# Linear attention: decay factors multiplied in place over 128 partitions, and half of each key tile copied by ScalarE

## The chip, the core and the metric

The program runs on one core of a Trainium2 chip. The metric is the device time of one execution in microseconds (us). Engines: PE is TensorE (matmuls; PEld its weight loads), DVE is VectorE, ACT is ScalarE, POOL is GpSimd, SP issues the DMAs.

## What is computed

Two blocks of a small model on 256 tokens of width 1024. The first block has two layers; each has three branches (softmax attention, pooling, gated linear attention), merged by gates. The change is in the linear attention, which the reference writes as a scan over chunks with a decay for each key dimension:

```python
def gla_scan(q, k, v, log_a, s0, with_out):
    ...
    def step(s, inp):
        qq, kk, vv, aa = inp
        b = jnp.cumsum(aa, axis=2)
        ...
        inter = jnp.einsum('bhcd,bhde->bhce', qq * jnp.exp(b), s)
        decay = jnp.exp(jnp.where(mask, b[:, :, :, None, :] - b[:, :, None, :, :], -jnp.inf))
        attn = jnp.einsum('bhid,bhjd,bhijd->bhij', qq, kk, decay)
        intra = jnp.einsum('bhij,bhje->bhie', attn, vv)
        return s_new, inter + intra

    _, o_f = gla_scan(q, k, v, af, sc_f, True)
    _, o_b = gla_scan(flip(q), flip(k), flip(v), flip(ab), sc_b, True)
```

There are 4 heads of 64 key dimensions and 128 value dimensions, a forward and a backward direction, and a context sequence of 256 tokens ahead of the 256 main ones.

## The kernel before

Activations lie transposed: 128 features on the partitions, tokens along the row (columns 0 to 255 the context, 256 to 511 the main sequence). Layer 0 works on all 512 columns, layer 1 on the main 256 alone (`lo` is 0 or 256). All large matmuls are three products of rounded halves: `split` has ACT cast a weight tile from `raw` to `wh` (L425) and DVE, or POOL for every fourth tile, subtract it to get `wl` (L427).

One head of linear attention (`gla_head`) puts both directions in one tile: partitions 0 to 63 hold the forward decay sums, 64 to 127 the backward ones (`U`, and `Rr` shifted by one token). The queries and keys of two heads share a tile (`q2`, `k2`), so a head's 64 rows are the upper or the lower half (`rows`). The causal product is cut in eight levels (`lv`): at each, every block of 2s tokens (s = 1 to 128) has an upper and a lower half, and queries of the one meet keys of the other. A level makes `E`, the exponentials of the distances to the block's middle (two subtractions on DVE, L1136 and L1137, and one exponential on ACT, L1138), and multiplies it with q and k into four quarters (L1140 to L1143): queries into `Z` (one of three buffers `zb`) and keys into `K_` (one of eight, `kz`), whose other quarters were set to zero once for each layer (L1187). Each multiplication covers 64 partitions and half the columns; two run on POOL and two on DVE:

```python
            ef.tensor_mul(v4(Z, 1, f), v4(E, 1, f), v4(qs, 1, rows))
            ef.tensor_mul(v4(K_, 0, f), v4(E, 0, f), v4(ks, 0, rows))
            ew.tensor_mul(v4(Z, 0, w_), v4(E, 0, w_), v4(qs, 0, rows))
            ew.tensor_mul(v4(K_, 1, w_), v4(E, 1, w_), v4(ks, 1, rows))
```

One level later `cross` multiplies `K_` with `Z` on PE (`plv`, L1111 and L1105) and DVE or ACT puts the product into place under a mask. At a head's start a product without decay (`pd`, L1081) and the state of the context (`ek`, L1066 to L1074, transposed on PE as `pst`, L1089) are made.

A head yields after each level, and `weave` puts the matmuls of the merge and of the pooling branch (`z_merge`, `pbr`, `z_pool_x`) between the yields. A scheduling layer then fixes one order for each engine; the engines take their instructions strictly in that order.

Of the kernel before, what the change touches and what calls it, by code (L numbers as in the profile page):

```python
# [674 lines left out]
def trunk(b, l, xs, st, A):  # L675

    nc, S = b.nc, b.S
# [4 lines left out]
    q0 = 0 if full else 256  # L682
# [16 lines left out]
    if st is None:  # L699
# [3 lines left out]
        for s_ in range(2):  # L703
            acc, t = S.cols(256), S.cols(256)
# [48 lines left out]
    def win2(name, t, cols):  # L753
        return win_pair((name, t), (name, t + 1), cols, cols)
# [6 lines left out]
    q2, k2, gv, la = [], [], [], []  # L761
# [131 lines left out]
    def silu2(ps):  # L893

        g = S.cols(NQ)
        nc.scalar.activation(g.ap, ps[:, QC], AF.Tanh, scale=0.5)
        nc.vector.scalar_tensor_tensor(g.ap, g.ap, 1.0, ps[:, QC], ALU.add, ALU.mult)
        return g
# [146 lines left out]

    def gla_head(hd):
        rows = slice(64 * (hd % 2), 64 * (hd % 2) + 64)
        qs, ks = q2[hd // 2], k2[hd // 2]
        U, Rr = la[hd], S.get()
        tot = b.sm.tile([P, 2], F32, tag="tot", name="tot")  # L1050
        A, Ao = S.get(), S.get()
        for s_ in range(2):
            c = slice(256 * s_, 256 * s_ + 256)
# [12 lines left out]
        ek = S.get()  # L1066
        nc.scalar.activation(ek[:, 0:256], U[:, 0:256], AF.Exp, bias=bias[:, 0:1], scale=b.c("sgn")[:, 0:1])
        nc.scalar.activation(ek[:, 256:512], U[:, 256:512], AF.Exp, bias=bias[:, 1:2], scale=b.c("sgn")[:, 2:3])
        for d in range(2):
            o = slice(64 * d, 64 * d + 64)  # L1070
            eng = nc.gpsimd if o == rows else nc.vector
            eng.tensor_mul(ek[o, 0:256], ek[o, 0:256], ks[rows, 0:256])
            eng.tensor_mul(ek[o, 256:512], ek[o, 256:512], qs[rows, 256:512])

        pd = b.pb.tile([P, 512], F32, tag="p", name="pd")
        tiles = [t for t in range(4) if t // 2 in seqs]
# [1 line left out]
        blocks = [(t, hb) for t in tiles for hb in range(2)]  # L1078
        for t, hb in blocks:
            j = slice(t * P + 64 * hb, t * P + 64 * hb + 64)  # L1080
            nc.tensor.matmul(pd[64 * hb:64 * hb + 64, t * 64:t * 64 + 64], ks[rows, j], qs[rows, j], start=True, stop=True)  # L1081
        Ad = Ao[:, lo // 2:256]
        nc.scalar.mul(Ad, pd[:, lo // 2:256], 2.0)
        yield
# [1 line left out]
        def state():  # L1086
            ps = b.pb.tile([P, 512], F32, tag="p", name="pst")
            for t in range(2):
                nc.tensor.transpose(ps[:, t * P:(t + 1) * P], ek[:, t * P:(t + 1) * P], b.ident)  # L1089
            nc.scalar.copy(ek[:, 0:256], ps[:, 0:256])  # L1090
            yield
            for t in range(2):
                nc.tensor.matmul(ps[:, 256:384], ek[:, t * P:(t + 1) * P], gv[t][:, hd * P:(hd + 1) * P],
                                 start=t == 0, stop=t == 1)
            nc.scalar.copy(ek[:, 0:P], ps[:, 256:384])
            yield

        def cross(lv):
            ps = b.pb.tile([P, 512], F32, tag="p", name="plv")
            Z, K_ = b.zb[lv % 3], b.kz[lv]  # L1100
            t64 = lambda t_: t_.rearrange("p (t i) -> p t i", i=64)
            if lv == 7:
                for t in tiles:
                    j = (t ^ 1) * P
                    nc.tensor.matmul(ps[:, t * P:(t + 1) * P], K_[:, j:j + P], Z[:, t * P:(t + 1) * P], start=True, stop=True)  # L1105
                nc.scalar.copy(Ao[:, lo:], ps[:, lo:])
                return
            for t, hb in blocks:
                j = t * P + 64 * hb
                i = j if lv < 6 else t * P + 64 * (1 - hb)  # L1110
                nc.tensor.matmul(ps[64 * hb:64 * hb + 64, t * 64:t * 64 + 64], K_[:, j:j + 64], Z[:, i:i + 64],  # L1111
                                 start=True, stop=True)
            src = ps[:, lo // 2:256]
            if lv < 6:
                mk = b.mask[:, lv * 64:(lv + 1) * 64].unsqueeze(1).broadcast_to((P, n // P, 64))
                nc.vector.copy_predicated(t64(Ad), mk, t64(src))
                src = Ad
            if lv > 4:
                for hb in range(2):
                    rr, o = slice(64 * hb, 64 * hb + 64), 64 * (hb if lv == 5 else 1 - hb)  # L1120
                    nc.scalar.copy(A[rr, lo:].rearrange("p (t i) -> p t i", i=P)[:, :, o:o + 64], t64(src)[rr])

        n = 512 - lo
        st_ = state()
        f, w_ = slice(0, 64), slice(64, 128)
        ef, ew = (nc.gpsimd, nc.vector) if hd % 2 == 0 else (nc.vector, nc.gpsimd)
        for lv in range(8):
            s = 1 << lv
            nb = n // (2 * s)
            E = S.get()  # L1130

            def v4(t_, half, o=slice(0, P)):
                return t_[o, lo:].rearrange("p (m h s) -> p m h s", h=2, s=s)[:, :, half]

            mid = Rr[:, lo:].rearrange("p (m c) -> p m c", c=2 * s)[:, :, s:s + 1].broadcast_to((P, nb, s))
            nc.vector.tensor_sub(v4(E, 0), mid, v4(U, 0))  # L1136
            nc.vector.tensor_sub(v4(E, 1), v4(U, 1), mid)  # L1137
            nc.scalar.activation(E[:, lo:], E[:, lo:], AF.Exp, scale=1.0 / TAU)  # L1138
            Z, K_ = b.zb[lv % 3], b.kz[lv]
            ef.tensor_mul(v4(Z, 1, f), v4(E, 1, f), v4(qs, 1, rows))  # L1140
            ef.tensor_mul(v4(K_, 0, f), v4(E, 0, f), v4(ks, 0, rows))
            ew.tensor_mul(v4(Z, 0, w_), v4(E, 0, w_), v4(qs, 0, rows))
            ew.tensor_mul(v4(K_, 1, w_), v4(E, 1, w_), v4(ks, 1, rows))  # L1143
            S.put(E)
            next(st_, None)
            if lv:
                cross(lv - 1)
            yield
        S.put(U, Rr)
        o_ = S.cols(NQ)  # L1150

        def tail():
# [29 lines left out]

    def gla_chain():
        gla_decay()
        b.kz, b.zb = [S.get() for _ in range(8)], [S.get() for _ in range(3)]
        for t in (*b.kz, *b.zb):
            nc.gpsimd.memset(t, 0.0)  # L1187
        yield
        outs, norm = [], iter(())
        for hd in range(4):  # L1190
            steps = gla_head(hd)
            while True:
                try:
                    next(steps)
                except StopIteration as e:
                    o_, norm = e.value
                    outs.append(o_)
                    break
                next(norm, None)
                yield  # L1200
        for _ in norm:
            yield
        S.put(*q2, *k2, *gv, *b.kz, *b.zb)
        for p2 in range(2):
            for i, ps in enumerate(win2("gla_gate", 2 * p2, QC)):
                g = silu2(ps)
                o_ = outs[2 * p2 + i]
                nc.vector.scalar_tensor_tensor(g.ap, o_.ap, 0.5, g.ap, ALU.mult, ALU.mult)  # L1208
                S.drop(o_)
                ygla.append(g)  # L1210
# [25 lines left out]

    weave(mla_chain(), 14, cat(mla_gates(), turns(mods(), gla_cols())), 15 if full else 11)
    weave(gla_chain(), 46, cat(merge(0, ymla), pooling(), merge(1, ypool)), 24)
    if full:
        b.lo_every = 1 << 30  # L1240
# [880 lines left out]
```

## Time and profile before

| | |
|---|---|
| three runs | 1535.64 us median (1535.45 to 1537.04) |
| the profiled execution | 1536.71 us, span 1534.9 us |
| busy share of the span | PE 93%, PEld 79%, DVE 70%, ACT 46%, POOL 28% |
| mean granted TensorE clock | 0.96 of full speed |
| linear attention with its filler | about 258 to 440 us (layer 0) and 770 to 925 us (layer 1) of the span |

The span runs from the first to the last instruction of the profiled execution. PE is busy nearly throughout, so what can move the time is where PE stands still or runs at a lower clock, and what the other engines do there.

### The profile page before, as it was taken

How to read it: one execution, taken by the hardware profiler on the slowest of the kernel's cores; microseconds unless marked ns; L12 is line 12 of the kernel's file. 1: busy time of each engine (PE TensorE's matmuls, PEld its weight loads, DVE VectorE, ACT ScalarE, POOL GpSimd, SP SyncE). 2: the span in 40 equal slices, each digit the busy share in tenths (PEclk: the TensorE clock that was granted, in tenths of full speed). 3: DMA queues.
4: the chain of work that ended last, by engine and by line, in shares of the span. 5: the costliest groups of instructions: out<-in, count | busy, mean ns of one | idle time of the engine just before them, and what ended most of it. 6: DMA issues, size and time to landing. Idle time of an engine off the chain costs nothing. (4 is left out here: it accounts for less than half of the span.)

```text
span 1534.9 us, 27423 instructions
## 1 busy us (share of the span) xinstructions
PE 1427.4 (93%) x10700; PEld 1212.0 (79%) x10700; DVE 1070.7 (70%) x2113; ACT 713.5 (46%) x1307; POOL 433.8 (28%) x428
## 2 busy tenths in 40 slices
PE   5999999999899999899998899979899999799997
PEld 1676776777788788886877789978668999699997
DVE  4455557877779865755589876758988549698843
ACT  3434445343433764454454445633532435366642
POOL 1010003445341004520035341344644003521212
PEclk8999999999999999999989999978999999799999
DMA  9534440321133363335024335844221325266660
GB/s 358 185 109 141 134 149 17 104 76 56 45 94 117 130 197 99 97 110 165 19 79 124 91 111 172 266 141 125 78 84 37 98 62 169 74 206 181 179 187 32
DMA packets 61041, 187.91 MB, mean 122 GB/s; under 512 B 7024, under 2 KB 8560, under 8 KB 60912
## 3 DMA queue, kind: packets, MB, share of 16 engines
q1 hardware_dynamic: 60912, 186.17, 38.5%
q8 instruction: 84, 1.38, 0.4%
q14 instruction: 45, 0.37, 0.1%
HBM read 180.11 MB, written 6.03 MB: 121 GB/s over the span
## 5 line engine op out<-in xcount | busy, mean ns | idle before, releaser
L425 ACT CAST wh<-raw 128x1024 fp32r<-128x1024 f32 (+1 forms) x296 | 279.4, 949 | 255.9 <-PE y L442 50.6
L427 DVE TENSOR_TENSOR wl<-raw,wh 128x1024 fp32r<-128x1024 f32 (+1 forms) x225 | 263.1, 1170 | 163.9 <-ACT wh L425 160.9
L427 POOL TENSOR_TENSOR wl<-raw,wh 128x1024 fp32r<-128x1024 f32 (+1 forms) x71 | 144.6, 2037 | 641.9 <-ACT wh L425 624.8
L442 PE MATMUL z_merge<-s,wh 128*128 128x512 f32 (+1 forms) x768 | 199.6, 350 | 0.0
L442 PEld LDWEIGHTS z_merge<-s,wh 128*128 128x128 f32 x768 | 135.5, 197 | 17.4 <-issue 1.5
L442 PE MATMUL z_merge<-s,wl 128*128 128x512 f32 (+1 forms) x384 | 133.0, 346 | 0.0
L442 PE MATMUL pbr<-s,wh 128*128 128x256 f32 (+1 forms) x512 | 120.6, 327 | 2.9 <-ACT s L432 2.0
L442 PE MATMUL pup<-s,wh 128*128 128x256 f32 x656 | 118.5, 283 | 0.1
L442 PEld LDWEIGHTS pup<-s,wh 128*128 128x128 f32 x656 | 102.5, 192 | 0.2 <-ACT wh L425 0.2
L442 PE MATMUL y<-s,wh 128*128 128x256 f32 x496 | 99.6, 297 | 0.0
L442 PEld LDWEIGHTS pbr<-s,wh 128*128 128x128 f32 x512 | 86.8, 192 | 12.3 <-ACT s L432 2.6
L442 PE MATMUL pwo<-s,wh 128*128 128x256 f32 (+1 forms) x448 | 91.4, 302 | 2.3 <-ACT s L1251 1.7
L442 PE MATMUL pup<-s,wl 128*128 128x256 f32 x328 | 92.8, 283 | 0.0
L442 PEld LDWEIGHTS y<-s,wh 128*128 128x128 f32 x496 | 79.8, 196 | 7.4 <-issue 4.9
L442 PE MATMUL pbr<-s,wl 128*128 128x256 f32 (+1 forms) x256 | 83.1, 325 | 0.0
L442 PEld LDWEIGHTS z_merge<-s,wl 128*128 128x128 f32 x384 | 75.9, 198 | 8.5 <-issue 0.8
L442 PEld LDWEIGHTS pwo<-s,wh 128*128 128x128 f32 x448 | 73.1, 194 | 5.5 <-ACT s L1251 1.9
L1138 ACT ACTIVATE s<-s 128x512 f32<-128x512 f32 (+1 forms) x64 | 33.3, 524 | 89.1 <-DVE s L1137 77.9
L442 PE MATMUL y<-s,wl 128*128 128x256 f32 x248 | 71.7, 289 | 0.0
L432 ACT CAST s<-s 128x256 fp32r<-128x256 f32 (+1 forms) x88 | 42.6, 487 | 57.1 <-DVE s L1208 14.3
L442 PE MATMUL pwo<-s,wl 128*128 128x256 f32 (+1 forms) x224 | 67.6, 302 | 1.5 <-DVE wl L427 1.5
L442 PE MATMUL pdn<-s,wh 128*128 128x256 f32 x352 | 63.4, 283 | 0.0
(490 smaller groups left out, 3545.7 us busy)
## 6 DMA issues: line engine op xcount, KB each, us to landing
raw<-wts SPq DMA_DIRECT2D x294, 512.0 KB, 4.3
s<-wts SPq DMA_DIRECT2D x57, 256.0 KB, 5.1
s5t<-s SPq DMA_DIRECT2D x16, 256.0 KB, 2.0
s<-s5t SPq DMA_DIRECT2D x16, 256.0 KB, 3.3
s<-xc SPq DMA_DIRECT2D x8, 256.0 KB, 5.3
x<-xc SPq DMA_DIRECT2D x8, 256.0 KB, 5.0
s<-tabs SPq DMA_DIRECT2D x4, 256.0 KB, 3.8
out<-s SPq DMA_DIRECT2D x8, 128.0 KB, 1.8
```

The costliest lines, as they stand in the source:

```text
L425: self.nc.scalar.copy(hi[:, :n], src)
L427: self.last_lo = eng.tensor_sub(lo[:, :n], src, hi[:, :n])
L432: self.nc.scalar.copy(hi, src)
L442: self.nc.tensor.matmul(ps, u, v[:, cols], start=start and n == 0, stop=stop and n == last)
L1138: nc.scalar.activation(E[:, lo:], E[:, lo:], AF.Exp, scale=1.0 / TAU)
```

## The change

The 64 rows of q and k that belong to a head are first copied by ACT into two full tiles: `KQ` has k on partitions 0 to 63 and q on 64 to 127, `QK` the other way round (four copies of 64 partitions for each head). A level then multiplies `E` in place over all 128 partitions, the one half of its columns with `KQ`, the other with `QK`, in two DVE instructions. `E` itself serves as `Z`; in the quarters that were zero it now holds products that the zeros of `K_` or the mask cancel. ACT copies the two key quarters from `E` into `K_`. POOL has no work left in the levels. The three `zb` buffers and their six memsets go; `E` is freed after the matmuls of its level. The four multiplications of `ek` (L1072, L1073) now read `KQ` and `QK`: DVE does the context half of the columns, POOL the main half. `pd` reads `KQ` and `QK` instead of `k2` and `q2`.

```diff
--- before.py
+++ after.py
@@ -1045,7 +1045,13 @@
 
     def gla_head(hd):
         rows = slice(64 * (hd % 2), 64 * (hd % 2) + 64)
-        qs, ks = q2[hd // 2], k2[hd // 2]
+        f, w_ = slice(0, 64), slice(64, 128)
+
+        KQ, QK = S.get(), S.get()
+        for t_, (a, c) in ((KQ, (k2, q2)), (QK, (q2, k2))):
+            for o, src in ((f, a), (w_, c)):
+                c0 = q0 if src is q2 else 0
+                nc.scalar.copy(t_[o, c0:], src[hd // 2][rows, c0:])
         U, Rr = la[hd], S.get()
         tot = b.sm.tile([P, 2], F32, tag="tot", name="tot")
         A, Ao = S.get(), S.get()
@@ -1068,9 +1074,9 @@
         nc.scalar.activation(ek[:, 256:512], U[:, 256:512], AF.Exp, bias=bias[:, 1:2], scale=b.c("sgn")[:, 2:3])
         for d in range(2):
             o = slice(64 * d, 64 * d + 64)
-            eng = nc.gpsimd if o == rows else nc.vector
-            eng.tensor_mul(ek[o, 0:256], ek[o, 0:256], ks[rows, 0:256])
-            eng.tensor_mul(ek[o, 256:512], ek[o, 256:512], qs[rows, 256:512])
+            kt_, qt_ = (KQ, QK) if d == 0 else (QK, KQ)
+            nc.vector.tensor_mul(ek[o, 0:256], ek[o, 0:256], kt_[o, 0:256])
+            nc.gpsimd.tensor_mul(ek[o, 256:512], ek[o, 256:512], qt_[o, 256:512])
 
         pd = b.pb.tile([P, 512], F32, tag="p", name="pd")
         tiles = [t for t in range(4) if t // 2 in seqs]
@@ -1078,7 +1084,7 @@
         blocks = [(t, hb) for t in tiles for hb in range(2)]
         for t, hb in blocks:
             j = slice(t * P + 64 * hb, t * P + 64 * hb + 64)
-            nc.tensor.matmul(pd[64 * hb:64 * hb + 64, t * 64:t * 64 + 64], ks[rows, j], qs[rows, j], start=True, stop=True)
+            nc.tensor.matmul(pd[64 * hb:64 * hb + 64, t * 64:t * 64 + 64], KQ[f, j], QK[f, j], start=True, stop=True)
         Ad = Ao[:, lo // 2:256]
         nc.scalar.mul(Ad, pd[:, lo // 2:256], 2.0)
         yield
@@ -1097,19 +1103,21 @@
 
         def cross(lv):
             ps = b.pb.tile([P, 512], F32, tag="p", name="plv")
-            Z, K_ = b.zb[lv % 3], b.kz[lv]
+            Z, K_ = Es.pop(0), b.kz[lv]
             t64 = lambda t_: t_.rearrange("p (t i) -> p t i", i=64)
             if lv == 7:
                 for t in tiles:
                     j = (t ^ 1) * P
                     nc.tensor.matmul(ps[:, t * P:(t + 1) * P], K_[:, j:j + P], Z[:, t * P:(t + 1) * P], start=True, stop=True)
                 nc.scalar.copy(Ao[:, lo:], ps[:, lo:])
+                S.put(Z)
                 return
             for t, hb in blocks:
                 j = t * P + 64 * hb
                 i = j if lv < 6 else t * P + 64 * (1 - hb)
                 nc.tensor.matmul(ps[64 * hb:64 * hb + 64, t * 64:t * 64 + 64], K_[:, j:j + 64], Z[:, i:i + 64],
                                  start=True, stop=True)
+            S.put(Z)
             src = ps[:, lo // 2:256]
             if lv < 6:
                 mk = b.mask[:, lv * 64:(lv + 1) * 64].unsqueeze(1).broadcast_to((P, n // P, 64))
@@ -1122,8 +1130,7 @@
 
         n = 512 - lo
         st_ = state()
-        f, w_ = slice(0, 64), slice(64, 128)
-        ef, ew = (nc.gpsimd, nc.vector) if hd % 2 == 0 else (nc.vector, nc.gpsimd)
+        Es = []
         for lv in range(8):
             s = 1 << lv
             nb = n // (2 * s)
@@ -1136,17 +1143,17 @@
             nc.vector.tensor_sub(v4(E, 0), mid, v4(U, 0))
             nc.vector.tensor_sub(v4(E, 1), v4(U, 1), mid)
             nc.scalar.activation(E[:, lo:], E[:, lo:], AF.Exp, scale=1.0 / TAU)
-            Z, K_ = b.zb[lv % 3], b.kz[lv]
-            ef.tensor_mul(v4(Z, 1, f), v4(E, 1, f), v4(qs, 1, rows))
-            ef.tensor_mul(v4(K_, 0, f), v4(E, 0, f), v4(ks, 0, rows))
-            ew.tensor_mul(v4(Z, 0, w_), v4(E, 0, w_), v4(qs, 0, rows))
-            ew.tensor_mul(v4(K_, 1, w_), v4(E, 1, w_), v4(ks, 1, rows))
-            S.put(E)
+            nc.vector.tensor_mul(v4(E, 0), v4(E, 0), v4(KQ, 0))
+            nc.vector.tensor_mul(v4(E, 1), v4(E, 1), v4(QK, 1))
+            K_ = b.kz[lv]
+            nc.scalar.copy(v4(K_, 0, f), v4(E, 0, f))
+            nc.scalar.copy(v4(K_, 1, w_), v4(E, 1, w_))
+            Es.append(E)
             next(st_, None)
             if lv:
                 cross(lv - 1)
             yield
-        S.put(U, Rr)
+        S.put(U, Rr, KQ, QK)
         o_ = S.cols(NQ)
 
         def tail():
@@ -1182,8 +1189,8 @@
 
     def gla_chain():
         gla_decay()
-        b.kz, b.zb = [S.get() for _ in range(8)], [S.get() for _ in range(3)]
-        for t in (*b.kz, *b.zb):
+        b.kz = [S.get() for _ in range(8)]
+        for t in b.kz:
             nc.gpsimd.memset(t, 0.0)
         yield
         outs, norm = [], iter(())
@@ -1200,7 +1207,7 @@
                 yield
         for _ in norm:
             yield
-        S.put(*q2, *k2, *gv, *b.kz, *b.zb)
+        S.put(*q2, *k2, *gv, *b.kz)
         for p2 in range(2):
             for i, ps in enumerate(win2("gla_gate", 2 * p2, QC)):
                 g = silu2(ps)
```

Three places in the engines' orders. Names such as `s_573_7299` are tiles of the common arena (slot and serial number).

POOL at the first head of layer 0, before: after two products of `ek` it multiplies the levels (L1140 queries, L1141 keys).

```order
L1072 TENSOR_TENSOR s_242_2231<-s_242_2231,s_78_521 64x256
L1073 TENSOR_TENSOR s_242_2231<-s_242_2231,s_133_1024 64x256
L1140 TENSOR_TENSOR s_234_2098<-s_243_2248,s_133_1024 64x256
L1141 TENSOR_TENSOR s_226_2090<-s_243_2248,s_78_521 64x256
L1140 TENSOR_TENSOR s_235_2099<-s_245_2313,s_133_1024 64x128x2
L1141 TENSOR_TENSOR s_227_2091<-s_245_2313,s_78_521 64x128x2
L427 TENSOR_TENSOR wl_2384<-raw_1_2113,wh_2383 128x512
L1140 TENSOR_TENSOR s_236_2100<-s_246_2334,s_133_1024 64x64x4
L1141 TENSOR_TENSOR s_228_2092<-s_246_2334,s_78_521 64x64x4
```

The same place after the change:

```order
L1079 TENSOR_TENSOR s_241_2231<-s_241_2231,s_236_2164 64x256
L1079 TENSOR_TENSOR s_241_2231<-s_241_2231,s_235_2163 64x256
L427 TENSOR_TENSOR wl_2384<-raw_1_2107,wh_2383 128x512
L427 TENSOR_TENSOR wl_2564<-raw_0_2437,wh_2563 128x512
L427 TENSOR_TENSOR wl_2763<-raw_1_2438,wh_2762 128x512
```

The level products are gone from POOL; of its work in the heads the `ek` products and the weight differences (L427) stay, and they stand next to each other.

ACT at the first head of layer 1, before: the exponentials of the state (L1067, L1068) and of the levels (L1138), the state's evacuations (L1090, L1095) and the casts of weights (L425).

```order
L1067 ACTIVATE s_572_7286<-s_550_7104,bias,cons 128x256
L1068 ACTIVATE s_572_7286<-s_550_7104,bias,cons 128x256
L1138 ACTIVATE s_573_7299<-s_573_7299 128x256
L1138 ACTIVATE s_575_7364<-s_575_7364 128x256
L1090 COPY s_572_7286<-pst 128x256
L1138 ACTIVATE s_576_7381<-s_576_7381 128x256
L425 CAST wh_7425<-raw_1_7169 128x512
L1095 COPY s_572_7286<-pst 128x128
```

After, where L1145 is the level's exponential, L1149 and L1150 are the copies into `K_`, L1096 and L1101 the state's evacuations:

```order
L1073 ACTIVATE s_576_7304<-s_555_7122,bias,cons 128x256
L1074 ACTIVATE s_576_7304<-s_555_7122,bias,cons 128x256
L1145 ACTIVATE s_577_7317<-s_577_7317 128x256
L1145 ACTIVATE s_579_7382<-s_579_7382 128x256
L425 CAST wh_7443<-raw_1_7181 128x512
L1149 COPY s_562_7164<-s_577_7317 64x128
L1150 COPY s_562_7164<-s_577_7317 64x128
L1096 COPY s_576_7304<-pst 128x256
L1149 COPY s_563_7165<-s_579_7382 64x64x2
L1150 COPY s_563_7165<-s_579_7382 64x64x2
L1145 ACTIVATE s_580_7399<-s_580_7399 128x256
L1101 COPY s_576_7304<-pst 128x128
```

A pair of copies stands behind each exponential, and the state's evacuation L1096 and the next casts stand behind the first pairs.

DVE at the same head, before: the levels' subtractions, the `ek` products (L1072, L1073) and the two quarters of each level that DVE multiplies here (L1142, L1143).

```order
L1136 TENSOR_TENSOR s_576_7381<-s_569_7225,s_550_7104 128x32x4
L1072 TENSOR_TENSOR s_572_7286<-s_572_7286,s_432_5939 64x256
L1137 TENSOR_TENSOR s_576_7381<-s_550_7104,s_569_7225 128x32x4
L1073 TENSOR_TENSOR s_572_7286<-s_572_7286,s_495_6480 64x256
L1142 TENSOR_TENSOR s_565_7154<-s_573_7299,s_495_6480 64x128
L1143 TENSOR_TENSOR s_557_7146<-s_573_7299,s_432_5939 64x128
L1142 TENSOR_TENSOR s_566_7155<-s_575_7364,s_495_6480 64x64x2
L1143 TENSOR_TENSOR s_558_7147<-s_575_7364,s_432_5939 64x64x2
L1142 TENSOR_TENSOR s_567_7156<-s_576_7381,s_495_6480 64x32x4
L1143 TENSOR_TENSOR s_559_7148<-s_576_7381,s_432_5939 64x32x4
L427 TENSOR_TENSOR wl_7396<-raw_1_7312,wh_7395 128x1024
```

After, where L1143 and L1144 are the subtractions, L1078 the `ek` products and L1146 and L1147 the multiplications in place:

```order
L1143 TENSOR_TENSOR s_580_7399<-s_573_7243,s_555_7122 128x32x4
L1078 TENSOR_TENSOR s_576_7304<-s_576_7304,s_571_7237 64x256
L1078 TENSOR_TENSOR s_576_7304<-s_576_7304,s_572_7238 64x256
L1144 TENSOR_TENSOR s_580_7399<-s_555_7122,s_573_7243 128x32x4
L1146 TENSOR_TENSOR s_577_7317<-s_577_7317,s_571_7237 128x128
L1147 TENSOR_TENSOR s_577_7317<-s_577_7317,s_572_7238 128x128
L1146 TENSOR_TENSOR s_579_7382<-s_579_7382,s_571_7237 128x64x2
L1147 TENSOR_TENSOR s_579_7382<-s_579_7382,s_572_7238 128x64x2
L427 TENSOR_TENSOR wl_7414<-raw_1_7330,wh_7413 128x1024
```

DVE has as many instructions for each level as before, over 128 partitions where there were 64, and both `ek` products that the transposes wait for now stand on it.

## Rows read from the trace of the kernel before

**Rows 1.** The page, part 1: busy us (share) and instructions of TensorE.

```profile
PE 1427.4 (93%) x10700; PEld 1212.0 (79%) x10700; DVE 1070.7 (70%) x2113; ACT 713.5 (46%) x1307; POOL 433.8 (28%) x428
```

**Rows 2.** Windows: the two attention stretches (us busy per engine, PEclk, DMA share, GB/s).

```profile
258.00:440.00 182.00, 170.17 (x1138) 137.27 (x1134) 144.70 (x258) 73.85 (x131) 86.25 (x96) 0.97 0.23 70
...
770.00:925.00 155.00, 136.95 (x1128) 125.67 (x1125) 130.32 (x304) 78.84 (x164) 62.91 (x88) 0.91 0.34 103
```

**Rows 3.** Windows of 5 us in layer 1, the same columns.

```profile
790.00:795.00 5.00, 3.21 (x19) 2.35 (x21) 4.50 (x8) 2.92 (x6) 4.24 (x7) 0.59 0.00 0
820.00:825.00 5.00, 0.20 (x2) 0.01 (x1) 4.77 (x16) 2.67 (x6) 0.45 (x1) 1.00 0.57 156
825.00:830.00 5.00, 4.83 (x23) 4.86 (x24) 4.63 (x13) 1.85 (x6) 2.13 (x4) 0.51 0.63 193
855.00:860.00 5.00, 1.49 (x8) 1.28 (x9) 4.90 (x10) 2.58 (x8) 3.26 (x3) 0.92 0.57 150
```

**Rows 4.** Waits of PE in 250 to 480 us: total, times, longest (us).

```profile
PE plv L1111 <- POOL s L1141: 5.5, 3, 3.2
...
PE plv L1111 <- POOL s L1143: 1.7, 1, 1.7
```

**Rows 5.** Timeline of DVE, layer 1: start us, us, engine, line, out<-in.

```profile
787.27 0.28 DVE L1136 TENSOR_TENSOR s<-s,s 128x128 f32<-128x128 f32 x1
...
788.35 0.82 DVE L1137 TENSOR_TENSOR s<-s,s 128x128 f32<-128x128 f32 x1
...
794.42 0.29 DVE L1143 TENSOR_TENSOR s<-s,s 64x128 f32<-64x128 f32 x1
```

**Rows 6.** Timeline of POOL at the same place.

```profile
788.20 0.82 POOL L1072 TENSOR_TENSOR s<-s,s 64x256 f32<-64x256 f32 x1 [16.56 <-ACT s L1067]
```

**Rows 7.** Groups by form, DVE, 770 to 930 us: busy, mean ns, idle before.

```profile
L427 DVE TENSOR_TENSOR wl<-raw,wh 128x1024 fp32r<-128x1024 f32 x23 | 29.6, 1288 | 12.4 <-ACT wh L425 12.1
L1137 DVE TENSOR_TENSOR s<-s,s 128x128 f32<-128x128 f32 x32 | 13.1, 409 | 0.1
L1136 DVE TENSOR_TENSOR s<-s,s 128x128 f32<-128x128 f32 x32 | 11.4, 358 | 1.7 <-PE pbr L442 1.1
L1140 DVE TENSOR_TENSOR s<-s,s 64x128 f32<-64x128 f32 x16 | 8.5, 530 | 0.5
...
L1141 DVE TENSOR_TENSOR s<-s,s 64x128 f32<-64x128 f32 x16 | 6.8, 427 | 2.3 <-ACT s L1138 1.0 <-ACT s L1166 0.5
...
L1142 DVE TENSOR_TENSOR s<-s,s 64x128 f32<-64x128 f32 x16 | 6.4, 400 | 1.0
...
L1143 DVE TENSOR_TENSOR s<-s,s 64x128 f32<-64x128 f32 x16 | 5.6, 352 | 0.6
```

**Rows 8.** Groups by form, POOL, 770 to 930 us.

```profile
L1143 POOL TENSOR_TENSOR s<-s,s 64x128 f32<-64x128 f32 x16 | 10.0, 633 | 11.1 <-ACT s L1138 11.0
L1140 POOL TENSOR_TENSOR s<-s,s 64x128 f32<-64x128 f32 x16 | 10.0, 630 | 13.8 <-PE plv L1111 5.9 <-ACT s L1138 3.9 <-issue 3.6
L1141 POOL TENSOR_TENSOR s<-s,s 64x128 f32<-64x128 f32 x16 | 9.9, 623 | 7.2 <-ACT s L1138 7.2
L1142 POOL TENSOR_TENSOR s<-s,s 64x128 f32<-64x128 f32 x16 | 9.4, 590 | 9.3 <-PE plv L1111 5.5 <-ACT s L1138 3.2
```

**Rows 9.** Groups by form, ACT, 250 to 500 us.

```profile
L1121 ACT COPY s<-s 64x256 f32<-64x256 f32 x8 | 3.2, 403 | 6.2 <-DVE s L1116 6.2
```

**Rows 10.** Groups by form, ACT, 770 to 930 us.

```profile
L1138 ACT ACTIVATE s<-s 128x256 f32<-128x256 f32 x32 | 13.1, 416 | 32.9 <-DVE s L1137 23.0 <-DVE tot L1057 4.9 <-DVE s L1058 3.8
...
L1059 ACT COPY s<-s 128x510 f32<-128x510 f32 x4 | 2.5, 614 | 3.0 <-DVE s L1142 1.8 <-DVE s L1143 0.9 <-DVE s L1054 0.2
...
L1121 ACT COPY s<-s 64x128 f32<-64x128 f32 x8 | 2.4, 296 | 1.8 <-DVE s L1116 1.7
```

**Rows 11.** Timeline of POOL, later in layer 1.

```profile
855.51 2.35 POOL L427 TENSOR_TENSOR wl<-raw,wh 128x1024 fp32r<-128x1024 f32 x1 [4.24 <-ACT wh L425]
```

**Rows 12.** Timeline of DVE, at that place.

```profile
855.58 2.43 DVE L1137 TENSOR_TENSOR s<-s,s 128x128 f32<-128x128 f32 x1
```

## The prediction

> **What bounds the kernel now.** I read the page's busy shares first, then the windows of the two attention stretches, then PE's waits there, and last the timeline of the engines that PE waits for.
>
> PE is busy for 93% of the span [rows 1], so the time is PE's work plus its gaps and what it loses to a lower clock. In layer 0's stretch PE stands still for 182 - 170.2 = 11.8 us and the granted clock is 0.97, which costs 0.03 x 182 = 5.5 us of full speed; in layer 1's it stands still for 155 - 137.0 = 18.0 us at a clock of 0.91, another 14 us [rows 2]. Together 49 us: more than that the change cannot give, unless it shortens PE's own work, and it leaves every matmul in its place or a few rows from it. Lower clocks stand behind gaps: 4.8 us of standstill at 820, then 0.51 (that is, 1.2 GHz for nearly all of the next 5 us) [rows 3].
>
> Who makes PE wait? In layer 0 it is mostly POOL: waits of 5.5 and 1.7 us end with a level's second product there, L1141 or L1143 [rows 4]. In layer 1 it is DVE: in four slices with gaps, 20 us in all, PE is busy 9.7 us and DVE 18.8 us [rows 3]. DVE is busy for 130 of 155 us there, ACT for 79, POOL for 63 [rows 2]. So DVE is the engine to relieve in layer 1, and the reader should see that part of its business is not work. Alone, a subtraction of 128x128 takes 0.28 us and a product of 64x128 0.29 us; at 788.35, with a product of POOL in progress from 788.20 to 789.02, the same subtraction takes 0.82 us [rows 5, 6].
>
> **The change part by part.**
>
> *POOL's level products go.* That is 64 instructions of some 0.6 us in layer 1, 39.3 us together, of its 63 us [rows 8, 2]; 0.62 of what POOL does there.
>
> *DVE's level work.* Count and length stay: two products for each level, and a 128-partition instruction (0.28 us) costs what a 64-partition one (0.29 us) does [rows 5]. What goes is the stretching beside POOL. In layer 1 the 64 products take 8.5 + 6.8 + 6.4 + 5.6 = 27.3 us where 64 x 0.29 would be 18.6: 8.7 us too much. The 64 subtractions take 24.5 us where 64 x 0.28 is 17.9: 6.6 too much [rows 7, 5]. Products run beside POOL's products of the same level, so I take all of their 8.7 as returned; of the subtractions' 6.6 I take POOL's falling share, 0.62, that is 4.1. DVE gets back 13 us in layer 1. The rest stays, since POOL keeps its weight differences: at 855.51 one of 2.35 us holds a subtraction on DVE for 2.43 us [rows 11, 12].
>
> The rule for this is in the Trainium skill, SBUF — State Buffer, section "Who interferes with whom": a DVE instruction with two SBUF inputs and a GpSimd instruction that reads SBUF share a port, and whichever starts second waits for the whole of the other. The 2.43 us beside 2.35 agree. By that rule alone each removed product could give DVE back its whole length, 39 us in layer 1, three times what the rows' sums give; that result is one of the rivals.
>
> *Gain of PE in layer 0.* The waits on POOL's products are 7.2 of 11.8 us of standstill [rows 4, 2]. I take them as gone, and with them their share of the clock's loss, 7.2/11.8 x 5.5 = 3.4 us: 10.6 us.
>
> *Gain of PE in layer 1.* A microsecond off DVE ahead of a gap is one off the gap, as DVE is busy through the gaps (18.8 of 20 us). But relief that falls behind the gap, or ahead of a place where DVE waits for something else (12 us for weight casts alone [rows 7]), is lost. Bounds are 0 and 13 us plus its clock; I take three quarters of 13, 10 us, and nothing for the clock, as gaps get shorter here and do not go.
>
> *Copies into `K_` on ACT.* No row shows a copy of exactly this kind. The nearest, a copy within SBUF of 64x256 or 64x128, take 0.403 and 0.296 us [rows 9, 10]. Two for each of 32 levels are 25.8 us in layer 0 and 18.9 in layer 1. The copies into `KQ` and `QK`: 16 of 64x512 at 0.61 (the copy of 128x510 [rows 10]), 9.8 us, in layer 0; 8 such and 8 of 64x256, 4.9 + 3.2 = 8.1 us, in layer 1. So ACT goes from 74 to 110 of 182 us and from 79 to 106 of 155 us: it has the room, and in layer 1 it now stands idle for 32.9 us ahead of the levels' exponentials, waiting for DVE [rows 10]. On the path the copies take the place of POOL's second product (0.62 us in layer 1 [rows 8]) ahead of `plv`. What remains as a cost is the queue: behind a pair of copies, which waits for DVE's products, stand the state's evacuation L1096 and the next casts. I charge one pair a head, 4 x 0.8 + 4 x 0.6 = 5.6 us, and half of it to PE, as PE has filler and several cast tiles ahead: 3 us. Bounds: 0 (all hidden), and the rival below.
>
> *The rest* I cost at nothing. `pd` waits for the copies into `KQ` and `QK`, but these need only q and k and stand ahead of the head's chain on ACT; without that cover it is 4 x 0.61 = 2.4 us a head. The six memsets that go were done before the heads. `ek`: both products that the transposes need now stand on DVE, two instead of one, and each no longer beside a product of POOL's. The freed slots and the arena's shifted numbers move no wait that I can find.
>
> **Sum.** 10.6 + 10 - 3 = 17.6, say 18 us less. The profiled execution took 1536.7 us (span 1534.9 and 1.8 around it), 1.1 above the median of 1535.64, so against the median it is 1517.6; I predict 1517 us.
>
> **The rivals.**
>
> *More than that.* If DVE and POOL stop holding each other up, the gaps go nearly all, and the low clock behind them with them. Three quarters of the 49 us would be 37: 1499 us. For it: PE's gaps in layer 1 have DVE busy right through them, and the skill's rule gives DVE up to 39 us. Against it: POOL keeps the differences that hold DVE longest (2.43 us), and the head starts are chains over DVE, ACT and PE that the change leaves.
>
> *Hidden.* DVE gets its 13 us and more, and PE waits for what came next: the exponential, the transposes, DVE's own queue with the 1.3 us weight differences. Then the copies on ACT eat most of the gain in layer 0, and 0 to 6 us remain: about 1533. For it: most waits in layer 1 end with chains of several engines, none of which names POOL.
>
> *Slower: ACT's queue becomes the bound.* ACT takes its instructions in order. A pair of copies stands still until DVE has done both products, and DVE may have a weight difference of 1.3 us ahead of them; the casts behind it hold DVE's next weight difference, which in turn holds the next products. If each of 32 pairs holds the queue for 2 us, ACT is taken for 106 + 64 = 170 of 155 us in layer 1, 15 us more than there is, and for 110 + 64 = 174 of 182 in layer 0, where 8 us may still be gained: 7 us slower, 1543. It decides from about 1.9 us a pair; at 1.2 us ACT takes 144 us in layer 1, just what the forecast leaves for the stretch. For it: ACT and DVE already wait for each other, 33 and 12 us in layer 1 [rows 10, 7]. Against it: after the change two exponentials often stand ahead of two pairs of copies, so DVE's products are done while ACT still works.
>
> **How the numbers follow.** A run-to-run spread of 0.1% makes 0.2%, 3 us, what a measurement here can tell from no change. The forecast, 8 to 28 us less, gets 0.56; more than that 0.13; hidden 0.17, of which half within 0.2%; slower 0.14. Faster is 0.56 + 0.13 + 0.09 = 0.78, same 0.08, slower 0.14. The time is 1517 us. For 8 in 10 the range runs from 1498 (leaving out some 0.05 below) to 1536 (leaving out the slower case and a little of the hidden one).
>
> **What would show it.** POOL's busy time falls by about 40 us in layer 1 and more in layer 0; the mean of DVE's products goes to 0.29 us in layer 1 and that of its subtractions to little above 0.28; DVE's busy time there falls from 130 to about 117 us. ACT's rises by some 63 us in all. PE's waits for POOL's products are gone and the clock in layer 1 is above 0.91. I am wrong in the step on ACT if `plv`, `pst` or the casts wait for L1149 or L1150 for more than a few us; wrong in the step on layer 1 if DVE's busy time falls and PE's standstill there stays near 18 us.

## The result, and the profile after

The changed kernel takes 1518.62 us (median, 1516.14 to 1518.76); the kernel before, run in turn with it, 1536.34. The ratio is 0.987, with a 95% interval of 0.985 to 0.989: faster by 18 us, where 1517 us had been forecast. The profiled execution has a span of 1516.9 us at a mean clock of 0.96, as before. The page's part 1 (busy us, share and instructions) answers to [rows 1]:

```profile
PE 1427.2 (94%) x10700; PEld 1212.1 (80%) x10700; DVE 1023.7 (67%) x2113; ACT 777.4 (51%) x1469; POOL 337.1 (22%) x294
```

ACT has 64 us more, POOL 97 less, DVE 47 less. PE is busy as long as before; the 18 us are standstill that is gone: 1534.9 - 1427.4 = 107.5 us before, 1516.9 - 1427.2 = 89.7 after.

To compare stretches that hold the same work I cut the span at matmuls: layer 0's attention from the first `pd` to the first `z_gla_gate`, layer 1's from the last `pgate` to the last `po`. Windows of the kernel before, in the columns of [rows 2]: layer 0, the stretch from the first `pwo` to the last `pgate` between the two, and layer 1.

```profile
257.60:481.70 224.10, 212.27 (x1401) 172.35 (x1401) 176.00 (x330) 92.31 (x160) 94.20 (x103) 0.98 0.25 74
573.10:774.50 201.40, 190.84 (x1254) 160.29 (x1252) 119.63 (x249) 97.22 (x197) 59.05 (x64) 0.97 0.32 100
774.50:919.50 145.00, 126.95 (x1063) 117.82 (x1061) 124.19 (x292) 74.67 (x157) 61.19 (x84) 0.91 0.33 99
```

The same three windows of the changed kernel:

```profile
257.80:471.80 214.00, 209.58 (x1400) 169.68 (x1400) 147.16 (x335) 128.31 (x239) 35.05 (x39) 0.99 0.26 77
563.10:766.50 203.40, 195.32 (x1254) 164.91 (x1252) 120.01 (x248) 99.22 (x201) 58.17 (x61) 0.95 0.31 96
766.50:900.10 133.60, 122.00 (x1063) 113.58 (x1061) 107.40 (x293) 98.44 (x233) 26.54 (x20) 0.92 0.37 111
```

Layer 0's stretch is 10.1 us shorter, layer 1's 11.4, and the one between them, which the change does not touch, 2.0 longer: the same 1254 matmuls take 4.5 us more at a clock of 0.95 instead of 0.97.

PE's waits in layer 0 (total, times, longest), answering to [rows 4]. Nothing of POOL is left among them:

```profile
PE plv L1118 <- ACT s L1150: 2.3, 2, 1.9
PE ps_ss L461 <- ACT s L1173: 1.1, 1, 1.1
PE pd L1087 <- ACT s L1054: 0.4, 1, 0.4
...
PE plv L1118 <- ACT s L1149: 0.3, 1, 0.3
```

And in layer 1, where the starts of the heads (`pst`) make 7.8 of 11.6 us of standstill:

```profile
PE pst L1095 <- ACT s L1089: 4.0, 2, 2.4
PE pst L1095 <- DVE s L1078: 2.4, 1, 2.4
...
PE pst L1099 <- ACT s L1096: 1.4, 1, 1.4
PE plv L1118 <- ACT s L1150: 1.4, 1, 1.4
```

DVE's groups by form in layer 1 (766.5 to 900.1 us), answering to [rows 7]; L1143 and L1144 are now the subtractions, L1146 and L1147 the products:

```profile
L1146 DVE TENSOR_TENSOR s<-s,s 128x128 f32<-128x128 f32 x32 | 13.6, 425 | 2.4 <-ACT s L1145 2.3
L1147 DVE TENSOR_TENSOR s<-s,s 128x128 f32<-128x128 f32 x32 | 10.7, 334 | 0.0
L1144 DVE TENSOR_TENSOR s<-s,s 128x128 f32<-128x128 f32 x32 | 9.5, 297 | 0.0
L1143 DVE TENSOR_TENSOR s<-s,s 128x128 f32<-128x128 f32 x32 | 9.1, 284 | 3.4 <-PE pbr L442 3.3
```

The subtractions have come down to their 0.28 us. The products have not: most take 0.28 us, but a few are very long. The timeline of both engines shows one beside a weight difference on POOL, where [rows 11, 12] showed a subtraction:

```profile
829.39 2.38 POOL L427 TENSOR_TENSOR wl<-raw,wh 128x1024 fp32r<-128x1024 f32 x1 [8.51 <-DVE s L1143]
829.66 2.25 DVE L1146 TENSOR_TENSOR s<-s,s 128x128 f32<-128x128 f32 x1 [0.31 <-ACT s L1145]
831.84 0.28 DVE L1147 TENSOR_TENSOR s<-s,s 128x128 f32<-128x128 f32 x1
```

ACT's groups by form there, answering to [rows 10]. The idle time ahead of the exponentials (L1145) that ends with DVE has gone from 23.0 to 6.1 us; the copies into `K_` (L1149, L1150) take the time that was forecast:

```profile
L1145 ACT ACTIVATE s<-s 128x256 f32<-128x256 f32 x32 | 12.6, 416 | 6.3 <-DVE s L1144 6.1
L1150 ACT COPY s<-s 64x128 f32<-64x128 f32 x32 | 9.6, 299 | 2.2 <-DVE s L1147 1.4
L1149 ACT COPY s<-s 64x128 f32<-64x128 f32 x32 | 9.5, 298 | 6.6 <-DVE s L1146 6.3
```

### The profile page after: what moved, and what is told of

It is laid out like the page before. It is cut to its first block, busy times and chain, and to the rows that moved or that the text cites. A ratio compares the mean times of both kernels' runs of the same rounds, so it can differ in the third digit from the quotient of the medians.

```text
span 1516.9 us, 27308 instructions
## 1 busy us (share of the span) xinstructions
PE 1427.2 (94%) x10700; PEld 1212.1 (80%) x10700; DVE 1023.7 (67%) x2113; ACT 777.4 (51%) x1469; POOL 337.1 (22%) x294
## 5 line engine op out<-in xcount | busy, mean ns | idle before, releaser
L425 ACT CAST wh<-raw 128x1024 fp32r<-128x1024 f32 (+1 forms) x296 | 279.2, 949 | 247.0 <-PE y L442 50.6
L427 DVE TENSOR_TENSOR wl<-raw,wh 128x1024 fp32r<-128x1024 f32 (+1 forms) x225 | 260.1, 1157 | 185.0 <-ACT wh L425 182.7
L427 POOL TENSOR_TENSOR wl<-raw,wh 128x1024 fp32r<-128x1024 f32 (+1 forms) x71 | 147.4, 2076 | 755.8 <-ACT wh L425 708.7
L442 PE MATMUL pwo<-s,wh 128*128 128x256 f32 (+1 forms) x448 | 95.8, 312 | 2.3 <-ACT s L1258 1.7
L442 PEld LDWEIGHTS pwo<-s,wh 128*128 128x128 f32 x448 | 76.9, 204 | 5.5 <-ACT s L1258 1.9
L442 PEld LDWEIGHTS pup<-s,wl 128*128 128x128 f32 x328 | 63.0, 192 | 0.0
```

The costliest lines, as they stand in the source:

```text
L425: self.nc.scalar.copy(hi[:, :n], src)
L427: self.last_lo = eng.tensor_sub(lo[:, :n], src, hi[:, :n])
L442: self.nc.tensor.matmul(ps, u, v[:, cols], start=start and n == 0, stop=stop and n == last)
```

## The experiments

Theory: POOL's products stretch DVE's instructions; without them DVE's chain to PE gets shorter, and the copies on ACT cost little. Rivals: the gain is from POOL's queue being free, from buffers, from `ek`, or from the wider instructions. Ratios are to the kernel before, run beside each (its medians there lie between 1536.3 and 1538.9 us); lengths of the two attention stretches are cut as above.

| kernel | us | ratio, 95% interval | layer 0 | layer 1 |
|---|---|---|---|---|
| before | 1536.34 | 1 | 224.1 | 145.0 |
| after | 1518.62 | 0.987 (0.985 to 0.989) | 214.0 | 133.6 |
| 1 idle products on POOL | 1543.19 | 1.0031 (1.0013 to 1.0048) | 231.7 | 145.2 |
| 2 copies made twice | 1529.45 | 0.9946 (0.9927 to 0.9965) | 217.1 | 139.3 |
| 3 before, all products on DVE | 1524.44 | 0.9910 (0.9887 to 0.9932) | 215.3 | 138.5 |
| 4 `ek` as before | 1519.76 | 0.9869 (0.9835 to 0.9903) | 214.1 | 134.2 |
| 5 memsets on POOL | 1518.99 | 0.9861 (0.9831 to 0.9891) | 215.0 | 132.9 |
| 6 no differences on POOL | 1505.52 | 0.9778 (0.9764 to 0.9793) | 210.5 | 129.0 |
| 7 copies on POOL | 1513.63 | 0.9831 (0.9815 to 0.9848) | 211.5 | 128.3 |
| 8 before, five `zb` | 1541.76 | 1.0016 (1.0006 to 1.0026) | 230.5 | 141.3 |
| 9 edits 6 and 7 | 1505.73 | 0.9783 (0.9745 to 0.9821) | 211.6 | 124.7 |
| 10 no differences on POOL anywhere | 1490.60 | 0.9691 (0.9661 to 0.9721) | 211.8 | 129.2 |
| 11 edit 9, and `KQ`, `QK` on POOL | 1506.53 | 0.9783 (0.9744 to 0.9822) | 212.1 | 122.1 |
| 12 before, no differences on POOL | 1524.84 | 0.9904 (0.9873 to 0.9935) | 220.0 | 136.8 |

**1. Idle products on POOL.** The changed kernel, with two products for each level on POOL that nobody reads.

```diff
             nc.vector.tensor_mul(v4(E, 1), v4(E, 1), v4(QK, 1))
+            nc.gpsimd.tensor_mul(v4(b.dummy, 0, f), v4(KQ, 0, f), v4(QK, 0, f))
+            nc.gpsimd.tensor_mul(v4(b.dummy, 1, f), v4(KQ, 1, f), v4(QK, 1, f))
```

> The changed kernel, plus two products of 64 partitions a level on POOL into a tile that nobody reads: POOL's load as before the change, but nothing waits for it. Theory (DVE beside POOL is stretched, and in layer 1 that is the gain): DVE's products go from 0.33 to 0.42 us back to 0.4 and more, layer 1's stretch loses some 8 to 11 us of its 11.4 us gain, layer 0's a part, since there the waits ended on POOL's products themselves: 1528 to 1534 us. Rival (the gain is that POOL no longer stands on the path, stretching is harmless): 1519 to 1522 us.

The whole gain is gone, more than the theory had asked for. The windows of its two stretches:

```profile
256.20:487.90 231.70, 217.46 (x1402) 175.59 (x1401) 164.41 (x343) 132.12 (x243) 78.48 (x89) 0.95 0.22 72
781.60:926.80 145.20, 124.99 (x1063) 115.59 (x1062) 119.84 (x293) 98.59 (x233) 62.14 (x79) 0.90 0.32 103
```

And two groups by form of layer 1, the first of POOL's idle products and DVE's subtraction L1144:

```profile
L1148 POOL TENSOR_TENSOR s<-s,s 64x128 f32<-64x128 f32 x29 | 18.3, 631 | 20.1 <-ACT s L1054 18.2
...
L1144 DVE TENSOR_TENSOR s<-s,s 128x128 f32<-128x128 f32 x32 | 16.0, 500 | 0.0
```

DVE does the same work as in the changed kernel, yet is busy 17.3 us longer in layer 0 and 12.4 in layer 1; the stretches are 17.7 and 11.6 us longer. Here a microsecond on DVE is a microsecond of the stretch.

**5. Memsets on POOL.** The same place, but POOL only writes: three memsets of 128x512 for each level in layer 0, two in layer 1.

```diff
+            for _ in range(3 if full else 2):
+                nc.gpsimd.memset(b.dummy, 0.0)
```

> The changed kernel, plus three memsets a level (two in layer 1) on POOL into a tile that nobody reads: POOL is about as busy as before the change, some 80 us more, and has the same queue ahead of its weight differences and state products, but its added work only writes. Theory (DVE is stretched by products of POOL that read operands from SBUF as it does): time stays at 1517 to 1522 us and DVE's instructions keep their length. Rival (what took the gain away in the run with added products was POOL's queue, not the stretching): 1530 us or more.

No effect, and DVE's lengths are those of the changed kernel (groups of layer 1):

```profile
L1149 POOL MEMSET s<- 128x512 f32 x57 | 30.9, 543 | 3.1
...
L1144 DVE TENSOR_TENSOR s<-s,s 128x128 f32<-128x128 f32 x32 | 9.5, 298 | 0.0
```

The timeline there has two products of DVE that start while a memset runs and keep their 0.28 us:

```profile
789.85 0.52 POOL L1149 MEMSET s<- 128x512 f32 x1
789.86 0.28 DVE L1146 TENSOR_TENSOR s<-s,s 128x128 f32<-128x128 f32 x1
790.06 0.28 DVE L1147 TENSOR_TENSOR s<-s,s 128x128 f32<-128x128 f32 x1
```

POOL's memsets take 30.9 us in layer 1, not far from the 36 us of idle products. So it is neither POOL's queue nor its being busy that costs: it is POOL reading operands. In the Trainium skill, SBUF — State Buffer, section "Who interferes with whom", a DVE instruction with two SBUF inputs contends with a GpSimd instruction that reads SBUF and not with one that only writes; L1144's means of 500 ns in the kernel with idle products and 298 in the one with memsets agree.

**3. Before, all products on DVE.** The kernel before with `ef = ew = nc.vector`: four narrow products for each level, all on DVE, nothing on ACT.

> The kernel before with all four products of a level on DVE, in their old form of 64 partitions, none on POOL. POOL stops stretching DVE and leaves the path, but DVE gets 64 more products a layer, 27 us in layer 0 and 19 us in layer 1, about what the stretching took. Theory (DVE is the bound of layer 1, POOL's products of layer 0): layer 0 gains some 5 us, layer 1 nothing or loses a few: 1528 to 1538 us. Rival (it is enough that POOL is out of the levels): 1518 to 1523 us.

Missed (the time lies between the two forecasts): taking POOL out is by itself worth 0.991, two thirds of the whole change. Its window of layer 1:

```profile
767.20:905.70 138.50, 123.42 (x1063) 114.02 (x1062) 128.69 (x356) 74.52 (x157) 25.75 (x20) 0.94 0.33 104
```

DVE is busy for 128.7 us there, 4.5 more than in the kernel before, and the stretch is 6.5 shorter. So DVE's busy time alone does not set the stretch. I take it that what counts is how soon a level's chain of subtraction, exponential and products gets through, half of which had run on a slower and a waiting POOL; that was not measured by itself.

**7. Copies on POOL.** The changed kernel with the `K_` copies moved from ACT.

```diff
-            nc.scalar.copy(v4(K_, 0, f), v4(E, 0, f))
-            nc.scalar.copy(v4(K_, 1, w_), v4(E, 1, w_))
+            nc.gpsimd.tensor_copy(v4(K_, 0, f), v4(E, 0, f))
+            nc.gpsimd.tensor_copy(v4(K_, 1, w_), v4(E, 1, w_))
```

> The changed kernel with the copies into the key tiles on POOL instead of ACT, 45 us off ACT. Theory (whatever POOL reads stretches DVE, and ACT has room): slower than the change, 1524 to 1536 us, with DVE's products and subtractions longer again. Rival (copies of one operand do not disturb DVE, and ACT's queue costs some 9 us): 1508 to 1515 us.

Missed: it takes 1513.63 us where the changed kernel takes 1518.62, 5 less and not more. The half of the theory on DVE came out. Its subtractions in layer 1 are longer again (groups of experiment 7; 297 and 284 ns in the changed kernel), and DVE is busy 6.1 us longer in layer 0 and 2.4 in layer 1:

```profile
L1144 DVE TENSOR_TENSOR s<-s,s 128x128 f32<-128x128 f32 x32 | 11.8, 369 | 0.1
L1143 DVE TENSOR_TENSOR s<-s,s 128x128 f32<-128x128 f32 x32 | 11.5, 361 | 1.2 <-PE pbr L442 1.1
```

What failed is that this would decide the time. The timeline of both engines in layer 1 shows what one copy does to DVE:

```profile
800.58 0.28 POOL L1149 COPY s<-s 64x128 f32<-64x128 f32 x1 [1.96 <-DVE s L1146]
800.64 0.37 DVE L1146 TENSOR_TENSOR s<-s,s 128x128 f32<-128x128 f32 x1
...
801.81 1.21 DVE L427 TENSOR_TENSOR wl<-raw,wh 128x1024 fp32r<-128x1024 f32 x1
...
801.92 1.26 POOL L1150 COPY s<-s 64x128 f32<-64x128 f32 x1
```

A copy that starts first is short, and the product beside it takes 0.37 instead of 0.28 us and ends 0.15 us after the copy; one that starts beside a weight difference on DVE is itself held, 1.26 us, and DVE's 1.21 us stay as they are.

**2. Copies made twice.** Each pair of `K_` copies is issued a second time; ACT is busy for 819.8 us where it was 777.4.

> The changed kernel with each pair of copies into the key tiles done twice, 45 us more on ACT. Theory of the prediction (the copies cost PE 3 us in all): 1520 to 1523 us. Rival (ACT's queue is near to becoming the bound; in layer 1 it is busy 98 of 134 us and would be 117): 1528 us or more, with PE waiting for the copies and for the casts behind them.

The rival's time came: it costs 10.8 us (1529.45 - 1518.62). The two profiled executions lie 13.6 us apart: 3.1 and 5.7 in the two attention stretches, and 4.7 in the stretch between them, which has none of these copies. DVE's wait for the exponentials, which now queue behind the copies, is 7.0 us in layer 1 (8 waits), where it is 2.3 in the changed kernel. The row of DVE's waits in experiment 2:

```profile
DVE s L1146 <- ACT s L1145: 7.0, 8, 1.6
```

**4. `ek` as before.** In the changed kernel the four `ek` products are dealt to POOL and DVE by the head's parity again.

```diff
-            nc.vector.tensor_mul(ek[o, 0:256], ek[o, 0:256], kt_[o, 0:256])
-            nc.gpsimd.tensor_mul(ek[o, 256:512], ek[o, 256:512], qt_[o, 256:512])
+            eng = nc.gpsimd if o == rows else nc.vector
+            eng.tensor_mul(ek[o, 0:256], ek[o, 0:256], kt_[o, 0:256])
+            eng.tensor_mul(ek[o, 256:512], ek[o, 256:512], qt_[o, 256:512])
```

> The changed kernel with the products of the state dealt to DVE and POOL as before the change: the head's own half on POOL, the other on DVE. The prediction cost this edit at nothing: 1517 to 1521 us. Rival (the head starts gain because the transposes no longer wait for POOL): 1523 us or more, with the transposes waiting for POOL.

No effect.

**8. Before, five `zb`.** The kernel before with five buffers for `Z` instead of three, as the change lets a level keep its own tile.

> The kernel before with five buffers for the query tiles instead of three, and nothing else of the change. POOL's waits for PE's reads of a buffer (5.9 and 5.5 us in layer 1) go. Theory (buffers are not the cause): same as before, ratio 0.997 to 1.003. Rival (the change gains because its query tile comes from the arena and never waits): ratio 0.994 or less.

No gain in the time, so the buffers by themselves are not the cause. The trace is less even: layer 1's stretch is 3.7 us shorter than before and layer 0's 6.4 longer, and why layer 0 loses was not looked into.

**6. No differences on POOL in the attention stretches.** The changed kernel; the weight differences (L427) of these stretches all go to DVE.

```diff
+    b.lo_every = 1 << 30
     weave(gla_chain(), 46, cat(merge(0, ymla), pooling(), merge(1, ypool)), 24)
+    b.lo_every = 4
```

> The changed kernel with POOL's weight differences of the two attention stretches on DVE: 10 in layer 0 and 11 in layer 1, 17 and 20 us off POOL, 8 and 9 us more on DVE, which loses the stretching that is left (5 and 7 us over 0.42 and 0.28 us an instruction). Theory (a us of POOL that reads costs DVE less than a us): DVE's busy time rises by some 5 us and the time is 1518 to 1525 us. Rival (a difference on POOL holds DVE for its whole 2.4 us, twice what it takes on DVE): 1510 to 1516 us.

Better than the theory and the rival, 13 us below the changed kernel, although DVE has more to do. All level operations are at their bare length now (DVE's groups, layer 1):

```profile
L1144 DVE TENSOR_TENSOR s<-s,s 128x128 f32<-128x128 f32 x32 | 9.6, 299 | 0.1
L1146 DVE TENSOR_TENSOR s<-s,s 128x128 f32<-128x128 f32 x32 | 9.2, 288 | 2.3 <-ACT s L1145 1.9
L1147 DVE TENSOR_TENSOR s<-s,s 128x128 f32<-128x128 f32 x32 | 9.2, 287 | 0.0
L1143 DVE TENSOR_TENSOR s<-s,s 128x128 f32<-128x128 f32 x32 | 9.2, 286 | 1.5 <-PE pbr L442 1.4
```

**12. The same edit to the kernel before.** It shows whether that gain belongs to the change.

> The kernel before, with no differences on GpSimd in the attention stretches; its products on GpSimd stay. Theory that GpSimd's products and its differences hurt VectorE one beside the other: about the same 13 us as in the changed kernel, 1521 to 1527 us. Rival: while the products run on GpSimd, VectorE's operations beside them stay long whatever becomes of the differences, and VectorE gets 1.2 us of work for each difference moved to it: 1530 to 1537 us.

It does not: 0.9904 by itself, beside 0.987 for the change by itself, and 0.9778 for both; 0.9904 x 0.987 is 0.9775. Within the intervals the two gains add. L1137's mean falls from 409 [rows 7] to 325 ns here, with POOL's products still there.

**9 and 11. Copies on POOL too.** Edits 6 and 7 together, and then the copies into `KQ` and `QK` on POOL as well.

> The changed kernel with both of the last two edits: no differences (the halves subtracted) on GpSimd in the attention stretches, and the K_ copies on GpSimd. If the two gains have separate causes (VectorE held by GpSimd's differences; products and weight loads queued behind the copies on ScalarE), they add: 1518.6 - 13 - 5 is about 1500, 1496 to 1503 us. If both won back the same idle time of TensorE, it stays at about 1505 us, or a little more since GpSimd's copies lengthen VectorE's products.

> As the first of these kernels, with the copies of KQ and QK on GpSimd too. If ScalarE's queue is what is left in the way, 2 to 5 us below the first one (1493 to 1500 us); if GpSimd's queue or its longer copies now come last, 2 to 8 us above it.

Neither is below experiment 6, as the second forecast for experiment 9 said; of the two for experiment 11 neither came. Yet layer 1's stretch is 4.3 and 6.9 us shorter than there. Windows of experiment 9, from the first `pwo` to the last `pgate`, and layer 1:

```profile
559.90:765.70 205.80, 197.51 (x1253) 166.87 (x1252) 119.98 (x249) 99.77 (x202) 56.05 (x60) 0.94 0.29 95
765.70:890.40 124.70, 119.36 (x1063) 111.00 (x1061) 108.64 (x302) 79.54 (x168) 41.13 (x75) 0.95 0.37 120
```

In experiment 6 the stretch before layer 1 took 203.5 us, with 192.8 us of PE at 0.96. Over the whole span experiment 9 has 4.5 us less standstill and 4.9 us more of PE's busy time for the same matmuls: in these two executions, what the attention gained was given back elsewhere, with a granted clock of 0.94 in the stretch before layer 1. The mean clock of the span does not settle it: the profiled execution of experiment 6 had 0.970, and its other three, at 0.964 to 0.965, took no longer. Why the clock is lower in stretches with the same work stays open.

**10. No differences on POOL anywhere.** The changed kernel with `lo_every = 1 << 30` throughout; two differences that the code pins to POOL remain.

> The changed kernel with no differences on GpSimd in any stretch. Theory that a difference on GpSimd costs VectorE its whole length everywhere: the stretches outside attention gain too, 1497 to 1504 us. Rival: there TensorE waits for VectorE hardly at all, so nothing more comes of it: 1503 to 1508 us, as with the attention stretches alone.

Better than the theory's range, and the best of all: 28 us below the changed kernel. The attention stretches are as in experiment 6, so the other 15 us come from elsewhere, 13 of them from 941.6 to 1283.9 us, the second block. There (window of experiment 10):

```profile
941.60:1283.90 342.30, 318.45 (x3371) 279.65 (x3369) 263.75 (x476) 146.74 (x283) 98.16 (x104) 0.95 0.37 119
```

In experiment 6 this work took 355.4 us, in the changed kernel 359.1, with 327.1 us of PE at 0.92. PE's standstill there falls from 32.0 us in the changed kernel to 23.9, and its waits that end with DVE from 16.3 to 8.0. The weight differences on DVE over the whole span, by form, experiment 10:

```profile
L427 DVE TENSOR_TENSOR wl<-raw,wh 128x1024 fp32r<-128x1024 f32 x226 | 278.2, 1235 | 169.8 <-ACT wh L425 168.2 <-PE pbr L442 0.8 <-DMA raw<-wts 0.3
L427 DVE TENSOR_TENSOR wl<-raw,wh 128x512 fp32r<-128x512 f32 x68 | 46.7, 687 | 15.0 <-ACT wh L425 14.8
```

The same view of the changed kernel:

```profile
L427 DVE TENSOR_TENSOR wl<-raw,wh 128x1024 fp32r<-128x1024 f32 x184 | 232.0, 1262 | 174.3 <-ACT wh L425 172.3 <-PE pbr L442 0.8
L427 DVE TENSOR_TENSOR wl<-raw,wh 128x512 fp32r<-128x512 f32 x41 | 28.1, 686 | 10.6 <-ACT wh L425 10.5
```

DVE does 69 differences more, 324.9 us instead of 260.1, and is busy over the span for 1026.1 us where it was 1023.7. So 65 us of work cost it 2.4. The lengths of all its other instructions add up to 54 us less, and instructions that overlap their neighbour account for some 8 us: beside those 69 on POOL it had lost most of what it takes to do them.

## Why the prediction came out

**The sum** of 18 us was 17.7 in the medians. Of its terms, one was right, one was right by two errors that cancel, and one was too small. The measured gains of the two stretches contain what the copies cost PE there. Together they are 21.5 us, where the sum had 10.6 + 10 - 3 = 17.6, and the rest of the span took 3.5 us more, for which the sum had no term. That the total fits is in part luck.

**PE in layer 0, 10.6 us: measured 10.1.** Standstill fell by 7.4 us, from 11.8 to 4.4. The 7.2 us of waits for POOL's products are gone, as counted; 2.6 us of waits for the copies have come, and 2.7 of other waits have gone. PE's busy time fell by 2.7 where 3.4 had been counted for the clock.

**PE in layer 1, 10 us: measured 11.4, by another route.** Standstill fell by 6.5 us only; PE's busy time fell by 5.0, where the clock had been counted at nothing. The step "a microsecond off DVE ahead of a gap is one off the gap" holds for a stretched DVE (experiment 1), but not for DVE's busy time as such (experiment 3, busier and faster). And the sizes behind the 13 us were not those: the 64 products gave back 3.0 us of the 8.7 (27.3 to 24.3), the subtractions 5.9 where 4.1 had been taken. The step that was mis-sized is "I take all of their 8.7 as returned": in the trace of the kernel before, 5.3 of those 8.7 us are four products that stand beside a weight difference on POOL, which the change leaves. One of them, in layer 1 before:

```profile
817.24 1.28 POOL L427 TENSOR_TENSOR wl<-raw,wh 128x512 fp32r<-128x512 f32 x1 [0.27 <-ACT wh L425]
817.27 1.40 DVE L1141 TENSOR_TENSOR s<-s,s 64x128 f32<-64x128 f32 x1
```

After the change five products are held so, for 5.6 us too much, and no subtraction; without the differences both are at 0.29 us (experiment 6). So the sign "the mean of DVE's products goes to 0.29 us" did not come. The rest of DVE's 16.8 us less is hardly in the lengths of its other operations, which add up to 0.8 us less. It is 7 us of overlap: instructions that follow each other without a wait start 0.20 us apart at a length of 0.28 (789.86 and 790.06 in experiment 5), and 238 of 292 instructions do so after the change, 157 of 291 before.

**Local clock gains are not net gains.** The two stretches together save 7.6 us of PE's busy time, but over the span it is 0.2. The net 18 us is standstill alone. Of the prediction's 3.4 us of clock, 2.7 were seen where they had been put; over the span all of it was lost again. That the change causes this loss is not shown: the stretch between the two layers takes between 201.4 us (before) and 208.1 us (experiment 2) in the thirteen traces that leave its work as it was, and its 2.0 us more after the change lie within that.

**ACT's copies, 3 us: too small.** Moving them off ACT gains 5 us (experiment 7), although they then lengthen DVE's instructions, and making them twice costs 8.8 us in the two stretches (experiment 2). PE's waits that end with L1149 or L1150 are 2.6 us in layer 0 and 1.4 in layer 1, together more than the charge, and at the "few us" that had been named as a sign against this step. The charge had counted the state's evacuation and the casts behind the pair, and left out the exponentials. DVE's waits for them in the two stretches are 7.9 us in the changed kernel, 5.3 with the copies on POOL and 16.7 with the copies made twice. So part of the cost stands under other names than the copies' own; how much of it reaches PE was not measured.

**Nothing for `ek`** was right (experiment 4). The rest of the list was not tried one by one; the buffers alone bring nothing (experiment 8).

**Put together**, from before to after: POOL's products to DVE, 0.991 (experiment 3); the rest of the change, above all two wide products in place instead of four narrow ones, with the copies on POOL, on to 0.9831 (experiment 7; what the wider products are worth by themselves was not tried); the copies to ACT, back to 0.987. The intervals allow some 4 us on each step. The rival "more" was not reached by the change, since it left POOL's differences in place, the reason given against it, and DVE got back 16.8 us in layer 1, not up to 39; with the differences gone everywhere (experiment 10) 1490.6 us is below its 1499.

## What to carry to other kernels

Before work is shared between VectorE and GpSimd, compare one two-operand VectorE instruction alone with the same one beside GpSimd: here 0.28 us became up to 2.4, and taking the weight differences off GpSimd paid although VectorE got more to do. Look for the cost of a new instruction on an in-order engine under the names of what stands behind it too, not only under its own. Cut two traces at the same matmuls and compare TensorE's busy time and its standstill apart, over the whole span, before a shorter stretch is booked as gain.

## What was unexpected of the hardware

- A weight difference of 128x1024 takes 1.2 us on DVE. On POOL it takes 2.4, and a 0.28 us instruction of DVE that starts beside it takes 2.3 to 2.4. To hand these to POOL relieved DVE of next to nothing, and without 69 of the 71 the kernel is 28 us faster.
- POOL writing alone (memsets, 30.9 us in layer 1) left the mean of a DVE subtraction at 298 ns; POOL reading two operands (35.6 us more) made it 500.
- POOL's copies of 64x128, with one operand and 0.28 us when nothing holds them, lengthened a product of DVE by 0.09 us only. That is the copy's shorter time and not its one operand: in the pairs shown, DVE's instruction ends 0.14 to 0.15 us after POOL's whatever POOL does, a product (789.02 and 789.17 us, [rows 5, 6]), a weight difference (831.77 and 831.91) or a copy (800.86 and 801.01).
